# Transposing attention probabilities with VectorE blocks and DMAs instead of TensorE in a two-layer hybrid decoder kernel

## Chip, cores and metric

One core of a Trainium2 chip runs the whole program. The time is that of one execution on the device, in microseconds (us); lower is better. Engines are named as the profile names them: PE is TensorE (PEld its weight loads), DVE is VectorE, ACT is ScalarE, POOL is GpSimd, SP is SyncE, which issues the loads of weights.

## What is computed

Two layers over 256 tokens of width 1024, in float32. Each layer is a half-step feed-forward block, a mixer of three gated branches, and a second half-step feed-forward block, each between RMS norms. The attention of the mixer, cut to what matters:

```
p_s = masked_softmax(q_rot @ k_slc * scale, m_s);  o_s = p_s @ v_slc     # 8 heads of 64, causal
p_w = masked_softmax(q_rot @ k_win * scale, m_w);  o_w = p_w @ v_win
y_nsa = g0 * o_c + g1 * o_s + g2 * o_w             # o_c: over 15 compressed blocks
p_m = softmax(q_m @ k_mem * scale);  y_mem = p_m @ v_mem                 # 4 heads of 128, 256 tokens
merged = g_conv*(y_conv @ w_conv) + g_nsa*(y_nsa @ w_nsa) + g_mem*(y_mem @ w_mem)
```

With 256 tokens and 64-token blocks, the 16 selected blocks are all blocks and the window covers all tokens, so `o_s` and `o_w` are both plain causal attention.

## The kernel before

Tokens are two tiles of 128 (t = 0, 1), each a `stream` that walks feed-forward, mixer, feed-forward for both layers. A product of float32 accuracy is three matmuls of "float32r" parts (`mm3`, L335): high by high, low by high, high by low. So every weight tile (128x1024, 512 KB, loaded by SP into `raw`) is split by ACT into `whi` and by DVE into `wlo` (`split_unit`, L266), and every moving or stationary activation is split too (`evac_split`, L368).

The order is a program of steps. A step is one piece of weight product of one stream, six matmuls in most cases; streams take turns, with t = 0 at most LEAD = 3 steps ahead. `advance` (L318) counts steps, runs what `later` deferred, and splits weights whose use is up to AHEAD = 4 steps off. Beside the streams, up to LANES = 4 chains (`background`, L1132) each advance one piece per step at most: compression, memory, and attention. A chain's `yield n` means: go on n steps later. The scheduler of the tile framework then places instructions within each engine by their readiness; SP's order is as written. Buffers come from rotating pools, `gtile` (19 of 128x1024) and `ttile` (8 of 128x520).

An attention chain has 512 score columns per PSUM bank and two banks. Per layer there are two `nsa_first` (t = 0; 128 keys, both variants of four heads), four `nsa_second` (t = 1; 256 keys, one variant of four heads) and two `mem_attention` (two heads, both t). Each puts its scores on PE, takes the maximum on DVE and the exponent on ACT, multiplies by the reciprocal sum and gate on DVE (L811, L840, L1044), and then needs the probabilities with keys on partitions. For that, PE transposes four 128x128 blocks into a PSUM bank (L779, L1053), ACT and DVE evacuate and split them (`ph`, `pl`), and PE multiplies by the values (L857, L1062). That happens twice in a chain: 32 groups of four transposes in the program. A fifth piece for t = 1 (third for t = 0), `cmp_attention`, adds the compressed branch; the last piece to arrive closes `o`, which ACT and DVE split into `ynsa` (L861). The mixer's branches come in the order convolution, memory, nsa (ORDER), and a stream that needs `ynsa` is held by `("until", ...)` (L1202) until its closing piece has been written into the program.

The feed-forward blocks already transpose without PE, in `turn_beside` (L385): DVE transposes 32x32 blocks, four DMAs issued by POOL write them to DRAM, one DMA brings them back rearranged, ACT and DVE split the result. The steps at which this is written are set by `AWAY, BACK, SPLIT = 1, 3, 8`.

Of the kernel before, what the change touches and what calls it, by code (L numbers as in the profile page):

```python
# [55 lines left out]
DBUFS = 4  # L56
CMP = 4
ATT_A, ATT_B, ATT_C, ATT_D = 1, 3, 2, 3
# [64 lines left out]
def program(nc, pools, a, out, plan):  # L123
# [261 lines left out]
    def turn_beside(src, n, put):  # L385
        c, f = n // P, n // 4
        blocks = gtile("blocks")
# [10 lines left out]
        def back():  # L398
            moved.append(gtile("moved"))
            nc.gpsimd.dma_start(moved[0][:, :n], there[:, :n])  # L400

        def split():
            hi, lo = gtile("turnhi", F32R), gtile("turnlo", F32R)
            dims, r = [[32, c], [f, 4], [1, 32]], "p (c q i) -> p c q i"
            hv, lv = hi[:, :n].rearrange(r, c=c, q=4), lo[:, :n].rearrange(r, c=c, q=4)
            nc.scalar.copy(hv, view(moved[0], 0, dims))  # L406
            nc.vector.tensor_sub(lv, view(moved[0], 0, dims), f32(hv))  # L407
            put(hi, lo)
# [3 lines left out]
        later(SPLIT, split)  # L412
# [234 lines left out]
    def kv_first(t, l, ps, r):  # L647
# [14 lines left out]
        def turn():  # L662
# [54 lines left out]
    def q_part(t, l, ps, r):  # L717
# [18 lines left out]
        def turn(i):  # L736
            def go():
                for half in range(2):
# [29 lines left out]
    def softmax_part(s3, dg, sums, c0, p3):  # L768
# [4 lines left out]
        for i in range(n):  # L773
            nc.scalar.activation(p3[:, i], s3[:, i], AF.Exp, bias=nm[:, i:i + 1], accum_out=sums[:, c0 + i:c0 + i + 1])
# [9 lines left out]
    def weighted_values(t, l, kt, var, g, ph, pl, last):  # L784
        vh, vl = values(kt, var, g)
        accumulate(t, l, 1, [(st, mv[:, :512]) for st, mv in ((vh, ph), (vh, pl), (vl, ph))], last)

    def nsa_first(l, g):
# [3 lines left out]
        pu = []  # L792
        for u in range(2):
# [7 lines left out]
            yield ATT_A  # L801
            s4 = s.rearrange("p (c k) -> p c k", c=4)
            p = ttile("p")
            p4 = p[:, :512].rearrange("p (c k) -> p c k", c=4)
            softmax_part(s4, s4, sums, u * 4, p4)
            pu.append(p4)
        yield ATT_B
        r = recip_gate(sums, 8, view(S["gt"][0], g * 12 + 1, [[3, 4], [1, 2]]))
        for u in range(2):
            for c in range(4):  # L810
                nc.vector.tensor_scalar(pu[u][:, c], pu[u][:, c], r[:, u * 4 + c:u * 4 + c + 1], None, op0=OP.mult)  # L811
        yield ATT_C
        for var in range(2):
            ph, pl = turn_probabilities([pu[h // 2][:, h % 2 * 2 + var] for h in range(4)])
            yield ATT_D
            weighted_values(0, l, 0, var, g, ph, pl, True)

    def nsa_second(l, var, g):
# [4 lines left out]
        pu = []  # L823
        for u in range(2):
# [7 lines left out]
            p = ttile("p")  # L832
            p3 = p[:, :512].rearrange("p (i k) -> p i k", i=2)
            softmax_part(s3, s3[:, :, P:2 * P], sums, u * 2, p3)
            pu.append(p3)
# [452 lines left out]
```

## Time and profile before

| | |
|---|---|
| time, median of 3 runs | 1289.2 us (1287.98 to 1293.4) |
| the profiled execution: time, span | 1287.19 us, 1285.4 us |
| PE busy, matmuls | 1273.1 us (99%), 6026 |
| DVE, ACT, POOL busy | 912.2 (71%), 738.6 (57%), 140.5 us (11%) |
| granted TensorE clock | 0.999 |
| moved by DMA | 263.81 MB, 205 GB/s |

The span is from the first to the last instruction; the execution's own time is 1.8 us longer. Busy shares of PE are modelled (matmuls overlap), so starts of matmuls tell more than busy time. The two layers lie one after the other: the attention chains stand at about 275 to 400 us and 910 to 1035 us.

### The profile page before, as it was taken

The numbers are of one execution on the slowest core, as the hardware profiler recorded it, in microseconds if no ns is written. First come the engines' busy times: TensorE is split into PE (matmuls) and PEld (weight loads), VectorE is DVE, ScalarE is ACT, GpSimd is POOL, SyncE is SP. The second block draws the span as 40 slices with busy tenths as digits, with TensorE's granted clock in tenths as the row PEclk, the third lists the DMA queues.
The fourth block names the chain that finished last, engine by engine and source line by source line (L and its number), as shares of the span: only waits on it lengthen the run. The fifth ranks groups of instructions, "written<-read, shape, count | busy, mean of one in ns | idle before, by whom it ended". The sixth has DMA issues, their size and how long they took to land.

```text
span 1285.4 us, 17101 instructions
## 1 busy us (share of the span) xinstructions
PE 1273.1 (99%) x6026; PEld 1055.2 (82%) x6026; DVE 912.2 (71%) x1352; ACT 738.6 (57%) x1175; POOL 140.5 (11%) x304
## 2 busy tenths in 40 slices
PE   9999999999999999999999999999999999999998
PEld 7888888888888888888888888888888888888886
DVE  6767467889877666676565765579997866766753
ACT  6655466886655464554464555568866555645541
POOL 3101401200000010111011011013000000110110
PEclk9999999999999999999999999999999999999999
DMA  8777585764555657787757776757654456577772
GB/s 265 245 248 252 188 271 172 220 213 131 151 155 161 206 180 199 254 257 244 231 175 240 220 248 229 240 167 233 184 151 144 132 180 211 179 216 236 254 247 81
DMA packets 126502, 263.81 MB, mean 205 GB/s; under 512 B 10097, under 2 KB 29201, under 8 KB 126417
## 3 DMA queue, kind: packets, MB, share of 16 engines
q1 hardware_dynamic: 118256, 239.30, 60.0%
q0 software_dynamic: 8128, 23.41, 5.4%
q8 instruction: 47, 0.77, 0.2%
q14 instruction: 39, 0.31, 0.1%
q10 hardware_dynamic: 32, 0.01, 0.0%
HBM read 250.10 MB, written 12.58 MB: 204 GB/s over the span
## 4 chain that ended last, share of the span: by engine, by line
PE 89%; DVE 4%; DMA 3%; ACT 2%; issue 1%; POOL 1%; DVEq 0%; POOLq 0%; ACTq 0%
PE acc L336 19%; PE acc L337 19%; PE acc L338 19%; PE y L338 6%; PE y L337 6%; PE y L336 6%; PE pt L379 2%; PE br L336 2%; PE br L337 2%; PE br L338 2%; PE o L857 1%; DMA there<-blocks 1%; DVE wlo L275 1%; PE pt L779 1%; DMA raw<-in_w_mix_in_dram 1%
## 5 line engine op out<-in xcount | busy, mean ns | idle before, releaser
L278 ACT ACTIVATE whi<-raw,gT 128x512 fp32r<-128x512 f32 (+2 forms) x432 | 364.5, 873 | 248.4 <-PE acc L338 167.1
L279 DVE SCALAR_TENSOR_TENSOR wlo<-raw,gT,whi 128x512 fp32r<-128x512 f32 (+2 forms) x432 | 396.4, 937 | 155.8 <-ACT whi L278 154.6
L336 PE MATMUL acc<-whi,hThi 128*128 128x512 f32 (+1 forms) x1184 | 464.1, 393 | 0.8 <-ACT hThi L370 0.8
L337 PE MATMUL acc<-wlo,hThi 128*128 128x512 f32 (+1 forms) x1184 | 458.5, 388 | 0.1
L338 PE MATMUL acc<-whi,hTlo 128*128 128x512 f32 (+1 forms) x1184 | 457.8, 388 | 0.0
L338 PEld LDWEIGHTS acc<-whi,hTlo 128*128 128x128 f32 x1184 | 222.2, 188 | 45.7 <-DVE hTlo L371 0.3
L336 PEld LDWEIGHTS acc<-whi,hThi 128*128 128x128 f32 x1184 | 222.4, 188 | 43.9 <-ACT hThi L370 1.6
L337 PEld LDWEIGHTS acc<-wlo,hThi 128*128 128x128 f32 x1184 | 222.6, 188 | 42.1 <-DVE wlo L279 0.6
L275 DVE TENSOR_TENSOR wlo<-raw,whi 128x1024 fp32r<-128x1024 f32 x144 | 175.2, 1222 | 79.3 <-ACT whi L274 78.0
L274 ACT CAST whi<-raw 128x1024 fp32r<-128x1024 f32 x144 | 150.3, 1051 | 104.9 <-PE acc L338 57.3
L337 PE MATMUL y<-wlo,turnhi 128*128 128x512 f32 x352 | 137.6, 391 | 0.1
L338 PE MATMUL y<-whi,turnlo 128*128 128x512 f32 x352 | 137.5, 391 | 0.0
L336 PE MATMUL y<-whi,turnhi 128*128 128x512 f32 x352 | 136.3, 390 | 0.0
L393 POOL DMA_DIRECT2D there<-blocks x96 | 53.0, 558 | 314.8 <-DVE blocks L388 312.0
L423 POOL TENSOR_TENSOR nr<-nv,mhalf 128x1 f32<-128x1 f32 x28 | 19.1, 682 | 545.4 <-DVE nv L421 541.4
L337 PEld LDWEIGHTS y<-wlo,turnhi 128*128 128x128 f32 x352 | 66.1, 188 | 14.4 <-DVE wlo L275 1.0
L338 PEld LDWEIGHTS y<-whi,turnlo 128*128 128x128 f32 x352 | 66.1, 188 | 13.5
L336 PEld LDWEIGHTS y<-whi,turnhi 128*128 128x128 f32 x352 | 66.0, 188 | 13.6
L407 DVE TENSOR_TENSOR turnlo<-moved,turnhi 128x1024 fp32r<-128x1024 f32 (+1 forms) x24 | 27.2, 1135 | 58.2 <-ACT turnhi L406 50.9
L406 ACT CAST turnhi<-moved 128x1024 fp32r<-128x1024 f32 (+1 forms) x24 | 23.4, 977 | 67.2 <-DMA moved<-there 44.6
L488 ACT ACTIVATE th<-acc,rs 128x512 f32<-128x512 f32 (+1 forms) x48 | 31.0, 645 | 17.5 <-PE acc L338 17.5
L493 DVE SCALAR_TENSOR_TENSOR wide<-th,rs,acc 128x512 f32<-128x512 f32 (+1 forms) x48 | 33.6, 701 | 2.9 <-DVE th L489 0.2
(292 smaller groups left out, 1232.6 us busy)
## 6 DMA issues: line engine op xcount, KB each, us to landing
raw<-in_ffn_w_in_dram SPq DMA_DIRECT2D x160, 512.0 KB, 4.8
raw<-in_w_mix_in_dram SPq DMA_DIRECT2D x96, 512.0 KB, 3.7
raw<-in_ffn_w_out_dram SPq DMA_DIRECT2D x88, 512.0 KB, 4.7
there<-blocks POOLq DMA_DIRECT2D x64, 128.0 KB, 5.2
moved<-there POOLq DMA_DIRECT2D x16, 512.0 KB, 5.8
raw<-in_ffn_w_in_dram SPq DMA_DIRECT2D x32, 256.0 KB, 4.0
raw<-in_w_mem_kv_dram SPq DMA_DIRECT2D x16, 512.0 KB, 4.9
raw<-in_w_mix_out_dram SPq DMA_DIRECT2D x16, 512.0 KB, 4.3
```

What stands on the lines that cost most here:

```text
L274: nc.scalar.copy(h, v)
L275: nc.vector.tensor_sub(w, v, f32(h))
L278: nc.scalar.activation(h, v, AF.Copy, scale=g)
L279: nc.vector.scalar_tensor_tensor(w, v, g, f32(h), op0=OP.mult, op1=OP.subtract)
L336: nc.tensor.matmul(ps, lhsT=xh, rhs=wh, start=start, stop=False, skip_group_check=skip)
L337: nc.tensor.matmul(ps, lhsT=xh, rhs=wl, start=False, stop=False, skip_group_check=skip)
L338: nc.tensor.matmul(ps, lhsT=xl, rhs=wh, start=False, stop=stop, skip_group_check=skip)
L379: nc.tensor.transpose(pt[:, j * P:(j + 1) * P], src[:, c0 + j * P:c0 + (j + 1) * P], ident)
L393: nc.gpsimd.dma_start(there[:, q * f:(q + 1) * f].rearrange("(p j) f -> j p f", j=32), blocks[q * 32:(q + 1) * 32, :n].rearrange("j (p f) ...
L407: nc.vector.tensor_sub(lv, view(moved[0], 0, dims), f32(hv))
L488: nc.scalar.activation(th[:, :n], pa[:, :n], AF.Tanh, scale=r_half)
L493: nc.vector.scalar_tensor_tensor(both[:, c0:c0 + n], th[:, :n], r2_half, pb[:, :n], op0=OP.mult, op1=OP.mult)
```

## The change

The probabilities of all three kinds of chain go through `turn_beside` in one 128x1024 tile per chain, and TensorE's 128 transposes for them are gone: 6026 matmuls become 5898. The scale by reciprocal sum and gate moves from DVE to ACT, as do the copies of `G` (`kv_first`) and `QT` (`q_part`) that DVE made. The split of the turned tile is written 10 steps after the block transpose (`ATT_T`), the products with the values 5 steps later (`ATT_D`). Chains of "nsa" and "memory" start at least 9 steps apart (`PACE`). The pool of DRAM buffers has 8 instead of 4.

```diff
-DBUFS = 4
+DBUFS = 8
-ATT_A, ATT_B, ATT_C, ATT_D = 1, 3, 2, 3
+ATT_A, ATT_B, ATT_C, ATT_D, ATT_T = 1, 3, 2, 5, 10
+CHAINS = 3, 5
+PACE, PACED = 9, ("nsa", "memory")
...
-                        eng = nc.scalar.copy if g == 0 else nc.vector.tensor_copy
+                        eng = nc.scalar.copy
...
-                    if half == 0:
-                        nc.scalar.copy(dst, pt)
-                    else:
-                        nc.vector.tensor_copy(dst, pt)
+                    nc.scalar.copy(dst, pt)
...
-    def turn_probabilities(parts):
-        pt = tbank()
-        for c, part in enumerate(parts):
-            nc.tensor.transpose(pt[:, c * P:(c + 1) * P], part, ident)
-        ph, pl = ttile("ph", F32R), ttile("pl", F32R)
-        evac_split(ph[:, :512], pl[:, :512], pt)
-        return ph, pl
...
+    def attend_values(t, l, parts):
+
+        def put(hi, lo):
+            def go():
+                for n, (half, kt, var, g) in enumerate(parts):
+                    ph, pl = [v[:, half * 512:(half + 1) * 512] for v in (hi, lo)]
+                    c = var * 512 + g * 128
+                    vh, vl = vz[kt][:, c:c + 128], vz[kt][:, c + 256:c + 384]
+                    accumulate(t, l, 1 / len(parts), [(vh, ph), (vh, pl), (vl, ph)])
+            later(ATT_D, go)
+        return put
...
     def nsa_second(l, var, g):
...
-        pu = []
+        p = gtile("p")
...
-        for h in range(4):
-            part = pu[h // 2][:, h % 2]
-            nc.vector.tensor_scalar(part, part, r[:, h:h + 1], None, op0=OP.mult)
+        for k in range(4):
+            part = view(p, k * P, [[512, 2], [1, P]])
+            nc.scalar.activation(part, part, AF.Copy, scale=r[:, k:k + 1])
         yield ATT_C
-        for kt in range(2):
-            ph, pl = turn_probabilities([pu[h // 2][:, h % 2, kt * P:(kt + 1) * P] for h in range(4)])
-            yield ATT_D
-            weighted_values(1, l, kt, var, g, ph, pl, kt == 1)
...
+        turn_beside(p, 1024, attend_values(1, l, [(kt, kt, var, g) for kt in range(2)]), ATT_T)
...
     def background():
-        while pending and len(lanes) < LANES:
+        while pending and len(lanes) < LANES and (pending[0][0][0] not in PACED or now[0] >= paced[0]):
             key, task = pending.pop(0)
+            if key[0] in PACED:
+                paced[0] = now[0] + PACE
             lanes.append([now[0], key, task])
```

`nsa_first` and `mem_attention` are changed in the same way (eight 128x128 scalings in the former). `turn_beside` itself keeps its work and gets a `wait` argument.

In the built program, **PE's queue** at the first chain of layer 0 before: the products of one half with the values (`o<-ph`), then the four transposes (`pt<-ident,p`) of the other half, between weight products.

```order
L338 MATMUL acc<-whi,hTlo 128x512
L857 MATMUL o<-ph,vz_123 128x512
L857 MATMUL o<-pl,vz_123 128x512
L857 MATMUL o<-ph,vz_123 128x512
L779 MATMUL pt<-ident,p 128x128 x4
L336 MATMUL acc<-whi,hThi 128x512
L337 MATMUL acc<-wlo,hThi 128x512
L338 MATMUL acc<-whi,hTlo 128x512
```

And with the change, at the products of the first chain:

```order
L804 MATMUL s<-KTh,QT_2375 128x256
L804 MATMUL s<-KTl,QT_2375 128x256
L856 MATMUL o<-turnhi,vz_123 128x512
L856 MATMUL o<-turnlo,vz_123 128x512
L856 MATMUL o<-turnhi,vz_123 128x512 x2
L856 MATMUL o<-turnlo,vz_123 128x512
L856 MATMUL o<-turnhi,vz_123 128x512
L338 MATMUL acc<-whi,hThi 128x512
L339 MATMUL acc<-wlo,hThi 128x512
L340 MATMUL acc<-whi,hTlo 128x512
```

The transposes are gone, and both halves' products stand together, right behind the scores (`s`) of the second chain.

**POOL's queue** before, at the end of the rotary embedding of t = 1 and at the convolution's small copies (`vT`, `carry`) up to the mixer's post-norm (`nr`):

```order
L725 TENSOR_TENSOR qr<-ra_2513,rb_2514 128x8x8
L726 TENSOR_TENSOR qr<-ra_2513,rb_2514 128x8x8
L1081 MEMSET vT 128x4x2
L1087 COPY carry<-vT 128x8
L1084 COPY vT<-carry 128x4x2
L423 TENSOR_TENSOR nr<-nv,mhalf 128x1 x2
```

With the change:

```order
L733 TENSOR_TENSOR qr<-ra_2513,rb_2514 128x8x8
L734 TENSOR_TENSOR qr<-ra_2513,rb_2514 128x8x8
L396 DMA there<-blocks 32x4x256 x4
L1077 MEMSET vT 128x4x2
L403 DMA moved<-there 128x1024
L396 DMA there<-blocks 32x4x256
L1083 COPY carry<-vT 128x8
L396 DMA there<-blocks 32x4x256 x3
L1080 COPY vT<-carry 128x4x2
L403 DMA moved<-there 128x1024
L396 DMA there<-blocks 32x4x256 x4
L403 DMA moved<-there 128x1024
```

Eight round trips of four DMAs out (`there`) and one back (`moved`) now stand in a queue that had nothing there but three small operations; the last of these three stands behind the first chain's way back, which waits for its way out.

**PE's queue** at the end of layer 0's attention before, where the nsa branch of t = 1 (`br<-whi,ynsa`) first meets its input; the closing product of that input stands 72 matmuls ahead of it:

```order
L338 MATMUL acc<-whi,hTlo 128x512
L336 MATMUL acc<-whi,hThi 128x512
L337 MATMUL acc<-wlo,hThi 128x512
L338 MATMUL acc<-whi,hTlo 128x512
L336 MATMUL br<-whi,ynsa 128x512
L337 MATMUL br<-wlo,ynsa 128x512
L338 MATMUL br<-whi,ynsa 128x512
L336 MATMUL br<-whi,ynsa 128x512
L337 MATMUL br<-wlo,ynsa 128x512
L338 MATMUL br<-whi,ynsa 128x512
```

With the change (`o<-phc` is that closing product, of the compressed branch; its four transposes `pt<-ident,pc` stand seven matmuls ahead of it, and 26 matmuls ahead of those the last of its scores):

```order
L340 MATMUL acc<-whi,hTlo 128x512
L338 MATMUL acc<-whi,hThi 128x512
L339 MATMUL acc<-wlo,hThi 128x512
L856 MATMUL o<-phc,vst 128x512
L340 MATMUL acc<-whi,hTlo 128x512
L338 MATMUL acc<-whi,hThi 128x512
L339 MATMUL acc<-wlo,hThi 128x512
L340 MATMUL acc<-whi,hTlo 128x512
L338 MATMUL br<-whi,ynsa 128x512
L339 MATMUL br<-wlo,ynsa 128x512
L338 MATMUL acc<-whi,hThi 128x512
L340 MATMUL br<-whi,ynsa 128x512
```

Four matmuls are left between the closing product and the first that needs its result.

## Rows read from the trace of the kernel before

**Rows 1.** The page: span, and each engine's busy time.
```profile
span 1285.4 us, 17101 instructions
...
PE 1273.1 (99%) x6026; PEld 1055.2 (82%) x6026; DVE 912.2 (71%) x1352; ACT 738.6 (57%) x1175; POOL 140.5 (11%) x304
```

**Rows 2.** Stretches: PE, PEld, DVE, ACT, POOL busy, clock, DMA share, GB/s.
```profile
225.00:275.00 50.00, 49.01 (x299) 42.08 (x298) 44.72 (x79) 41.41 (x82) 11.75 (x18) 1.00 0.78 238
...
275.00:345.00 70.00, 70.00 (x368) 58.48 (x367) 61.73 (x151) 48.32 (x123) 0.76 (x3) 1.00 0.48 142
345.00:430.00 85.00, 85.00 (x415) 70.81 (x414) 65.02 (x119) 48.64 (x87) 0.00 (x0) 1.00 0.56 161
...
465.00:640.00 175.00, 175.00 (x778) 145.00 (x777) 114.14 (x114) 88.44 (x97) 19.52 (x36) 1.00 0.74 232
```

**Rows 3.** Timeline of PE (start, us): first and last group of transposes.
```profile
290.61 0.39 PE L338 MATMUL acc<-whi,hTlo 128*128 128x512 f32 x1
290.84 0.60 PE L779 MATMUL pt<-ident,p 128*128 128x128 f32 x4
291.20 0.48 PE L336 MATMUL acc<-whi,hThi 128*128 128x512 f32 x1
291.51 0.40 PE L337 MATMUL acc<-wlo,hThi 128*128 128x512 f32 x1
...
1026.10 0.60 PE L779 MATMUL pt<-ident,p 128*128 128x128 f32 x4
```

**Rows 4.** Chain of waits, 275 to 430 us: shares, one group of transposes.
```profile
by line: PE acc L336 20.6%; PE acc L338 20.3%; PE acc L337 20.1%; PE br L336 6.2%; PE br L337 5.9%; PE br L338 5.9%; PE o L857 5.7%; PE pt L779 3.4%; PE s L829 2.4%; PE om L1062 1.8%; PE pt L379 1.5%; PE s L798 1.2%; PE pt L1053 1.1%; PE sc
...
291.00 0.44 PE pt L779 x4
```

**Rows 5.** Groups of PE by line: the removed transposes.
```profile
L779 PE MATMUL pt<-ident,p 128*128 128x128 f32 x96 | 14.4, 272 | 0.0
...
L1053 PE MATMUL pt<-ident,pm 128*128 128x128 f32 x32 | 4.8, 272 | 0.0
```

**Rows 6.** Groups of DVE by form: count, busy us, mean ns.
```profile
L388 DVE STREAM_TRANSPOSE blocks<-wide 128x1024 f32<-128x1024 f32 x16 | 19.8, 1237 | 0.0
L407 DVE TENSOR_TENSOR turnlo<-moved,turnhi 128x1024 fp32r<-128x1024 f32 x16 | 19.6, 1223 | 33.3 <-ACT turnhi L406 26.0 <-DMA there<-blocks 7.3
L371 DVE TENSOR_TENSOR pl<-pt,ph 128x512 fp32r<-128x512 f32 x24 | 16.4, 685 | 3.3 <-ACT ph L370 3.1
...
L840 DVE TENSOR_SCALAR p<-p,rg 128x256 f32<-128x256 f32 x32 | 9.3, 348 | 0.2
...
L811 DVE TENSOR_SCALAR p<-p,rg 128x128 f32<-128x128 f32 x32 | 6.9, 279 | 0.1
...
L974 DVE TENSOR_TENSOR sc<-sc,cmadd 128x128 f32<-128x128 f32 x4 | 1.1, 287 | 0.2
```

**Rows 7.** Groups of ACT by form, idle before each behind the bar.
```profile
L406 ACT CAST turnhi<-moved 128x1024 fp32r<-128x1024 f32 x16 | 16.8, 1048 | 33.8 <-DMA moved<-there 33.8
...
L774 ACT ACTIVATE p<-s,nm 128x256 f32<-128x256 f32 x32 | 14.9, 476 | 0.0
L370 ACT CAST ph<-pt 128x512 fp32r<-128x512 f32 x24 | 13.9, 580 | 14.4 <-PE pt L779 14.4
L774 ACT ACTIVATE p<-s,nm 128x128 f32<-128x128 f32 x32 | 11.4, 381 | 1.2 <-DVE nm L772 1.2
...
L406 ACT CAST turnhi<-moved 128x768 fp32r<-128x768 f32 x8 | 6.7, 836 | 33.3 <-issue 12.5 <-DMA moved<-there 10.8 <-DMA there<-blocks 10.0
```

**Rows 8.** Tile blocks: the DMA out, issue ns (min/median/max) and landing.
```profile
L393 POOL DMA_DIRECT2D there<-blocks x96: 552/552/641, 55.3 to 1229.2; - x96
...
DMA to landing us min/median/max: 2.8/5.0/7.4
```

**Rows 9.** Tile moved: the DMA back, likewise.
```profile
L400 POOL DMA_DIRECT2D moved<-there x24: 555/567/577, 62.6 to 1236.7; - x24
...
DMA to landing us min/median/max: 3.3/5.1/8.4
```

More of the change, by code (lines that the diff above doesn't have):

```diff
@@ L398, in back, with quarters, turn_beside, split @@
         def back():
-            moved.append(gtile("moved"))
+            moved.append(make("moved"))
             nc.gpsimd.dma_start(moved[0][:, :n], there[:, :n])
[L402 to L408, printed above, removed]
         later(AWAY, away)
         later(BACK, back)
-        later(SPLIT, split)
+        later(wait, lambda: finish(view(moved[0], 0, [[32, c], [f, 4], [1, 32]])))
+    def quarters(ap, c):
+        return ap if dry else ap.rearrange("p (c q i) -> p c q i", c=c, q=4)
+    def turn_beside(src, n, put, wait=SPLIT):
+        def split(mv):
+            hi, lo = gtile("turnhi", F32R), gtile("turnlo", F32R)
+            hv, lv = quarters(hi[:, :n], n // P), quarters(lo[:, :n], n // P)
+            nc.scalar.copy(hv, mv)
+            nc.vector.tensor_sub(lv, mv, f32(hv))
+            put(hi, lo)
+        turn(src, n, split, wait)
     def rstd(halves):
@@ L766, in values, with softmax_part @@
         return vz[t][:, c:c + 128], vz[t][:, c + 256:c + 384]
-    def softmax_part(s3, dg, sums, c0, p3):
+    def softmax_part(s3, dg, sums, place):
         n = s3.shape[1] if not dry else 1
@@ L852, in accumulate @@
         o = S["o"][t]
-        if last:
-            S["parts"][t] += 1
-        closing = last and S["parts"][t] == 5
+        S["parts"][t] += share
+        closing = S["parts"][t] == CHAINS[t]
         for n, (st, mv) in enumerate(products):
@@ L1018, in mem_attention @@
         scale = 128.0 ** -0.5
-        pm = []
+        p = gtile("pm")
+        sums = sp.tile([P, 4], F32, name="sumsm")
         for t in range(2):
@@ L1039, in mem_attention @@
         yield ATT_B
-        for p3, sums in pm:
-            r = sp.tile([P, 2], F32, name="rm")
-            nc.vector.reciprocal(r, sums)
-            for i in range(2):
-                nc.vector.tensor_scalar(p3[:, i], p3[:, i], r[:, i:i + 1], None, op0=OP.mult)
-        yield ATT_C
-        o = bank("om")
-        o3 = o.rearrange("p (i q) -> p i q", i=2)
-        for kt in range(2):
-            pt = tbank()
-            for i in range(2):
-                for t in range(2):
-                    c = i * 2 + t
-                    nc.tensor.transpose(pt[:, c * P:(c + 1) * P], pm[t][0][:, i, kt * P:(kt + 1) * P], ident)
-            ph, pl = ttile("phm", F32R), ttile("plm", F32R)
-            evac_split(ph[:, :512], pl[:, :512], pt)
-            yield ATT_D
-            vm = S["vm"][kt]
-            for i in range(2):
-                h = 2 * u + i
-                vh, vl = vm[:, h * P:(h + 1) * P], vm[:, 512 + h * P:512 + (h + 1) * P]
-                for n, (st, mv) in enumerate(((vh, ph), (vh, pl), (vl, ph))):
-                    nc.tensor.matmul(o3[:, i], lhsT=st, rhs=mv[:, i * 256:(i + 1) * 256],
-                                     start=(kt == 0 and i == 0 and n == 0), stop=(kt == 1 and i == 1 and n == 2),
-                                     skip_group_check=True)
@@ L1065, in mem_attention, with put, go @@
-        y = [t[:, u * 512:(u + 1) * 512] for t in S["ymT"]]
-        evac_split(y[0], y[1], o)
-        S["mparts"] += 1
-        if S["mparts"] == 2:
-            S["ymem"] = True
+        r = sp.tile([P, 4], F32, name="rm")
+        nc.vector.reciprocal(r, sums)
+        for k in range(4):
+            part = view(p, k * P, [[512, 2], [1, P]])
+            nc.scalar.activation(part, part, AF.Copy, scale=r[:, k:k + 1])
+        def put(hi, lo):
+            def go():
+                o = bank("om")
+                o3 = o.rearrange("p (i q) -> p i q", i=2)
+                for kt in range(2):
+                    ph, pl = [v[:, kt * 512:(kt + 1) * 512] for v in (hi, lo)]
+                    vm = S["vm"][kt]
+                    for i in range(2):
+                        h = 2 * u + i
+                        vh, vl = vm[:, h * P:(h + 1) * P], vm[:, 512 + h * P:512 + (h + 1) * P]
+                        for n, (st, mv) in enumerate(((vh, ph), (vh, pl), (vl, ph))):
+                            nc.tensor.matmul(o3[:, i], lhsT=st, rhs=mv[:, i * 256:(i + 1) * 256],
+                                             start=(kt == 0 and i == 0 and n == 0),
+                                             stop=(kt == 1 and i == 1 and n == 2), skip_group_check=True)
+                y = [t[:, u * 512:(u + 1) * 512] for t in S["ymT"]]
+                evac_split(y[0], y[1], o)
+                S["mparts"] += 1
+                if S["mparts"] == 2:
+                    S["ymem"] = True
+            later(ATT_D, go)
@@ L1071, in conv_part @@
+        yield ATT_C
+        turn_beside(p, 1024, put, ATT_T)
     def conv_part(t, l, u_s, c_ps, r):
```

55 lines of the change are left out of this document (23 added, 32 removed).

## The prediction

> **What bounds the kernel now.** Read the page's busy times first [rows 1]: PE is busy 1273.1 of 1285.4 us, DVE 71%, ACT 57%. As busy time of PE is modelled, check it where the change acts: in the table of stretches [rows 2] PE has no idle time from 275 to 430 us (70.00 of 70.00, 85.00 of 85.00), with DVE at 88% and 76% and the DMAs at about half, against 0.74 in a feed-forward stretch. Then look at starts [rows 3]: matmuls of 512 columns start 0.23 us apart (290.61, 290.84). This is the pitch of PE, and nothing but PE sets it. The chain of waits agrees [rows 4]: over these 155 us its shares all stand at PE lines. So in this stretch a microsecond of PE work removed is one gained, as long as what replaces it arrives in time.
>
> **What is removed from PE.** A group of four transposes starts at 290.84 us, the next matmul at 291.20, and the one after that at 291.51 instead of 0.23 us later [rows 3]: 0.36 + 0.08 = 0.44 us, which is also what the chain of waits gives such a group [rows 4]. The program loses 96 + 32 = 128 transposes [rows 5], in 32 groups from 290.84 to 1026.10 us [rows 3]: 32 x 0.44 = **14.1 us**. A second way to it: L779 and L1053 hold 3.4% + 1.1% of the 155 us [rows 4], 7.0 us a layer, 14.0 for two. No other matmul goes or comes.
>
> **What is moved between DVE and ACT, per layer.** DVE loses 16 scalings of 0.279 us, 16 of 0.348 and the memory chains' 8 (taken at 0.348 too), and 16 splits of 0.685; it gains 8 block transposes of 1.237 and 8 splits of 1.223 [rows 6]. 23.8 go, 19.7 come: -4 us, of some 127 busy in 275 to 430 us [rows 2]. ACT loses 16 evacuations of 0.580 and gains 8 of 1.048, 16 scalings of 128x128 (nearest row: the exponent of that size, 0.381) and 24 of 256 columns (0.476) [rows 7]: +17 us, on some 97 busy [rows 2]. 114 of the 148 us that would then be left is 77%: no new bound. The copies of `G` and `QT` that ACT takes over, 8 of at most 0.381 and 4 of about 0.58 [rows 7], add 5 us in 225 to 275 us, where ACT is busy 41.4 of 50 us [rows 2]. I cost this at nothing, since 8.6 us are idle there; if ACT's queue then holds up weight splits, PE's idle time there, now 1.0 us, may double, +1 us a layer.
>
> **What the new way costs, and what covers it.** One chain's round trip, by rows: block transpose 1.24 [rows 6], four issues of 0.55 on POOL = 2.2, landing 5.0 [rows 8], one issue 0.57, landing 5.1 [rows 9]: 14.1 us. Then 1.05 on ACT and 1.22 on DVE [rows 7, 6]: 16.4 us until PE may multiply. Against that stand ATT_T + ATT_D = 15 steps of six matmuls of 0.23 us, 20.7 us, and more where other chains' matmuls lie between. The cover leaves 4.3 us. With each landing the longest on record (7.4 and 8.4 us [rows 8, 9]) the way takes 22.1 us, 1.4 too many.
>
> What queues behind the new wait is the weight splits on ACT: the split of the turned tile is written 10 steps = 13.8 us after the block transpose, against 14.1 us, so ACT would stand 0.3 us at its head. The feed-forward blocks show that such a stand is free: their split comes after 8 steps = 11.0 us, so that by the same sum ACT should stand 3.1 us; its idle time there is (33.8 + 33.3) / 24 = 2.8 us [rows 7], and PE loses nothing by it (175.00 of 175.00 busy [rows 2]). On POOL a chain takes 2.2 + 5.0 + 0.57 = 7.8 us, and chains start 9 steps = 12.4 us apart, so round trips don't pile up. The convolution's copies (`vT`, `carry`) stand behind one such trip, at most 7.8 us later; between the transposes that feed them and the branch that needs them lie some 70 matmuls (16 us), so I cost this at nothing. DMA bytes rise by 16 x 1 MB where the DMAs are half idle [rows 2].
>
> The DMA issues themselves: 96 on POOL took 0.552 us in the median and 0.641 at most [rows 8], though DVE was busy most of the time beside them; by these rows five issues are 2.8 us a chain. [...]
>
> **The end of each layer's attention** is the tight place. Chains now start later and last longer, and the piece that closes `ynsa` for t = 1 comes right before its user: 26 matmuls (6.0 us) from the last compressed scores to their transposes, 7 (1.6 us) on to the product, 4 (0.9 us) on to the first use; before, 72 lay in the last gap. The first gap holds some 12 small dependent operations on DVE and ACT, at 0.287 each [rows 6] 3.4 us, plus 0.4 for the last matmul to end; but each can queue behind a weight split of 1.2 us, and two of these fill the gap. The second and third hold 0.58 on ACT and 0.685 on DVE each [rows 7, 6], with nothing to spare. So PE stands between 0 and 3 us a layer; I take 1.0, nearer to the lower end because the sums fit without queueing. **+2.0 us.**
>
> **The sum.** -14.1 + 2.0 = -12.1 us. The profiled execution took 1287.2 us, so 1275.1 against its own; the median of the runs shown is 2.0 us higher, so **1277 us** against that.
>
> **The rivals.**
> 1. *The ends of attention cost more*, 2 to 4 us a layer, because small operations queue behind two or three splits each: -14.1 + 6 = -8, 1281 us. For it: gaps of 4 and 7 matmuls. Against: DVE and ACT have idle time there.
> 2. *Nothing comes of it*, because DVE paces this stretch and not PE: 1289 us. For it: DVE at 88% in 275 to 345 us. Against: PE without idle time in the same stretch [rows 2], starts at pitch right behind a group [rows 3], and DVE loses work too.
> 3. *Slower: the products wait for the round trip.* Place: the first `o<-turnhi` of each of 16 chains. It decides from landings of 14.4 us together on (20.7 - 6.3 of fixed work); to eat the whole gain takes 12.1 / 16 = 0.76 us a chain, landings of 15.2 together against medians of 10.1. With all at their longest, 15.8, it is 16 x 1.4 = 22 us: 1277 + 22 = 1299. Against: the DMAs have less to do here than in the feed-forward stretches from which these landings come [rows 2].
> [...]
> That the change doesn't do what it says is excluded on PE by the order: 5898 matmuls, no transposes of `p` or `pm`.
>
> **How the numbers follow.** About 0.5% (6.4 us) can be told from no change. Forecast 0.70, its own range 1273 to 1280 (0 to 3 us a layer at the ends, and 1 us for what the medians of runs scatter); rival 1 0.14, of which 0.04 ends within 0.5%; rival 2 0.08; rival 3 0.06; rival 4 0.02. Faster by over 0.5%: 0.70 + 0.10, and 0.02 of rival 2 where it holds for one stretch only: 0.82. Within: 0.04 + 0.06 = 0.10. Slower: 0.08. The range reaches to 1284, which takes in rival 1, and down to 1272: the full 14.1 us and 3 more if PE's idle microseconds around DVE's removed work go too.
>
> **What would show it right or wrong.** Right: PE still without idle time in the attention stretch, no `pt<-ident,p`, ACT's idle before `turnhi` of attention under 2 us a chain, landings of `there` and `moved` near 5 us, and idle time of PE before `pt<-ident,pc`, `o<-phc` and `br<-whi,ynsa` of 0 to 3 us a layer. Wrong: PE waiting for `turnhi` or `turnlo` at `o` or `om`, POOL issues of over 1 us, ACT over 90% from 275 on, or weight matmuls that wait for `whi` behind an ACT that stands.

## The result, and the profile after

The changed kernel takes 1282.1 us (median of 14 runs, 1278.6 to 1286.3), the kernel before, run beside it, 1288.6 (14 runs, 1286.5 to 1293.4): a ratio of 0.994, 95% interval 0.9924 to 0.9957. It is faster, by about half of what was forecast: 6.5 us instead of 12.1. The time lies in the range of 1272 to 1284. The profiled execution took 1282.4 us, its span 1280.5.

Where the change acts, the forecast held. Three answers of the trace of after: the busy times of the page, the table of stretches (columns as in [rows 2]; the last is 5 us earlier than there), and the landing of the DMA out of `blocks` from 275 to 430 us.

```profile
PE 1259.4 (98%) x5898; PEld 1043.1 (81%) x5898; DVE 900.4 (70%) x1244; ACT 770.7 (60%) x1263; POOL 182.1 (14%) x384
```

```profile
225.00:275.00 50.00, 49.21 (x301) 42.43 (x300) 40.69 (x67) 44.50 (x92) 11.84 (x21) 1.00 0.78 241
275.00:345.00 70.00, 70.00 (x358) 58.93 (x357) 63.23 (x125) 60.29 (x150) 13.24 (x26) 1.00 0.71 221
345.00:430.00 85.00, 85.00 (x394) 69.78 (x393) 66.04 (x108) 54.08 (x97) 9.37 (x18) 1.00 0.71 213
460.00:635.00 175.00, 175.00 (x778) 145.04 (x777) 113.00 (x114) 86.94 (x96) 19.58 (x37) 1.00 0.74 234
```

```profile
DMA to landing us min/median/max: 2.3/3.3/5.4
```

PE is again without idle time from 275 to 430 us, with 128 matmuls fewer in the whole program; the DMAs have gone from half busy to 0.71, and their transfers land early all the same. ACT waits only 1.0 us in that stretch for its eight turned tiles, in all (groups by line, 275 to 430 us, of after):

```profile
L417 DVE TENSOR_TENSOR turnlo<-moved,turnhi 128x1024 fp32r<-128x1024 f32 x8 | 9.7, 1216 | 0.1
...
L416 ACT CAST turnhi<-moved 128x1024 fp32r<-128x1024 f32 x8 | 8.4, 1052 | 1.0 <-DMA moved<-there 1.0
```

To see where the rest went, the program is cut at five places that both kernels have: the last matmul ahead of the transposes of `x` with which a norm opens, where PE always waits 0.2 to 0.3 us. Between these starts of PE lie the stages; the first stage begins with PE's first transpose (`pt<-ident,first`), and the end is what comes after the start of the last matmul. In us, from the profiled executions (the runs below this line in the table are those of the experiments; "drain" is explained under the table):

| kernel | setup and ffn1, layer 0 | mixer 0 | ffn1, layer 1 | mixer 1 | end | GpSimd transfers | drain | median, runs |
|---|---|---|---|---|---|---|---|---|
| before | 206.9 | 246.8 | 207.0 | 246.5 | 6.3 | 138 | 2.80 | 1288.6, 14 |
| after | 208.1 | 239.0 | 211.3 | 238.9 | 11.3 | 218 | 9.17 | 1282.1, 14 |
| after, second trace | 213.8 | 238.9 | 212.1 | 239.1 | 11.3 | 218 | 9.17 | 1289.1, 1 |
| after, third trace | 208.7 | 238.9 | 210.1 | 240.1 | 11.3 | 218 | 9.17 | 1282.8, 6 |
| before, no transposes | 206.9 | 239.3 | 206.2 | 239.4 | 6.4 | 138 | 2.80 | 1272.3, 4 |
| before, 80 large transfers | 207.1 | 251.7 | 207.0 | 251.6 | 11.3 | 218 | 9.17 | 1303.9, 4 |
| before, 80 small transfers | 207.1 | 248.6 | 206.3 | 248.9 | 10.7 | 218 | 8.60 | 1295.5, 1 |
| after, writes by ScalarE | 207.7 | 247.8 | 206.3 | 246.7 | 6.8 | 154 | 4.11 | 1291.9, 10 |
| after, writes by SyncE | 210.8 | 244.2 | 206.3 | 247.8 | 6.7 | 154 | 4.11 | 1286.1, 10 |
| after, SPLIT 11 | 214.2 | 240.4 | 208.2 | 238.9 | 11.3 | 218 | 9.17 | 1287.7, 10 |
| after, ATT_T 6 | 209.5 | 259.4 | 214.5 | 259.4 | 11.5 | 218 | 9.17 | 1327.9, 1 |
| after, 30 small transfers | 210.5 | 239.1 | 206.3 | 240.1 | 13.2 | 248 | 11.05 | 1282.4, 12 |
| after, last roots moved | 207.3 | 239.1 | 208.5 | 240.1 | 6.4 | 218 | 9.15 | 1276.6, 6 |
| the same, constants by SyncE | 207.3 | 238.8 | 207.7 | 239.1 | 6.8 | 201 | 8.50 | 1272.5, 4 |

The two second feed-forwards (181.8 and 183.6 us) are the same in nearly all of them and are left out. From before to after: the mixers give 7.8 + 7.6 = 15.4 us, and 1.2 + 4.3 + 5.0 = 10.5 us are lost elsewhere, together 4.9, the difference of the spans.

**The end.** In both traces the queue of each of the five engines ends with DRAIN instructions and semaphore events, here called the closing barrier. The DRAINs on the queues of GpSimd and SyncE (durations in ns, minimum, median, maximum; start of the first and the last), of before and of after:

```profile
L1284 POOLq DRAIN  x3: 46/93/2803, 1280.4 to 1285.2; - x3
L1284 SPq DRAIN  x3: 7/7/7, 1284.6 to 1284.9; - x3
```

```profile
L1282 POOLq DRAIN  x3: 46/93/9170, 1270.6 to 1280.3; - x3
L1282 SPq DRAIN  x3: 7/7/7, 1274.8 to 1280.0; - x3
```

GpSimd's long DRAIN starts in both 1.3 us after the start of the last matmul, together with its last power. Before, it was over at 1283.2, ahead of SyncE, which reached the barrier at 1284.6. After, SyncE is there at 1274.8 and waits 5.0 us, until 1279.8.

**Layer 1's first feed-forward.** GpSimd's timeline of after in that stage (start, us; the idle time ahead and what ended it in brackets), and of before in layer 1's second feed-forward:

```profile
684.66 2.26 POOL L396 DMA_DIRECT2D there<-blocks  x4 [37.13 <-DVE blocks L391]
692.03 0.58 POOL L403 DMA_DIRECT2D moved<-there  x1 [5.11 <-PE acc L340]
695.59 2.20 POOL L396 DMA_DIRECT2D there<-blocks  x4 [2.97 <-issue]
703.29 0.56 POOL L403 DMA_DIRECT2D moved<-there  x1 [5.50 <-DMA there<-blocks]
```

```profile
1188.22 0.56 POOL L393 DMA_DIRECT2D there<-blocks  x1 [26.02 <-DVE blocks L388]
1191.39 1.65 POOL L393 DMA_DIRECT2D there<-blocks  x3 [2.60 <-issue]
```

"Issue" says that GpSimd waited for nothing that the profile shows; its blocks were written. Each kernel makes this pause of 2.4 to 3.0 us once where the trace lets it be told: the kernel before following its 119th transfer, the changed one following its 121st. The 40 additional transfers of layer 0 have moved it ahead by 496 us. What it does in after, from the timelines of PE, ACT and DVE, and the clock in the table of stretches:

```profile
709.55 0.39 PE L340 MATMUL acc<-whi,hTlo 128*128 128x512 f32 x1
710.15 1.04 ACT L416 CAST turnhi<-moved 128x1024 fp32r<-128x1024 f32 x1 [3.78 <-DMA moved<-there]
...
711.23 1.22 DVE L417 TENSOR_TENSOR turnlo<-moved,turnhi 128x1024 fp32r<-128x1024 f32 x1 [3.54 <-ACT turnhi L416]
...
712.37 0.74 DVE L501 SCALAR_TENSOR_TENSOR wide<-th,rs,acc 128x512 f32<-128x512 f32 x1
...
713.16 0.54 PE L338 MATMUL acc<-whi,hThi 128*128 128x512 f32 x1 [3.23 <-DVE wide L501]
```

```profile
705.00:709.50 4.50, 4.50 (x21) 3.74 (x20) 1.28 (x1) 1.15 (x1) 0.00 (x0) 1.00 0.91 320
...
713.20:717.00 3.80, 3.80 (x10) 2.98 (x11) 3.58 (x4) 1.15 (x1) 0.00 (x0) 0.55 0.12 24
```

The round trip that starts with blocks at 691.3 gets to its split 18.9 us later, with 8 steps (11 us) of cover; ACT and DVE stand at their queues' heads, the evacuation behind them doesn't come, and PE stands 3.2 us. Then the granted clock is 0.55: matmuls start 0.43 us apart (713.93, 714.36), and 10 go in 3.8 us where 16 or 17 would at the pitch of 0.23: another 1.5 us.

**The setup.** PE waits there for small constants that GpSimd loads between round trips: 0.4 us in before, 1.4, 5.2 and 1.7 us in the three traces of after. The first 1236 rows of PE's order are the same in both programs, and up to the first landmark the rows of all engines come in the same order in both traces, so no way is seen by which the change would reach this stage. The wait differs from run to run; but the four traces of kernels built from before have 206.9 to 207.1 us here, and the nine of kernels built from after that load these constants on GpSimd have 207.3 to 214.2. So chance alone isn't shown, and the cause stays open (the eight DRAM buffers instead of four were not tried by themselves).

### The profile page after: what moved, and what is told of

It reads as the page before. It is cut to its first block, busy times and chain, and to the rows that moved or that the text cites. A ratio compares the mean times of both kernels' runs of the same rounds, so it can differ in the third digit from the quotient of the medians.

```text
span 1280.5 us, 16988 instructions
## 1 busy us (share of the span) xinstructions
PE 1259.4 (98%) x5898; PEld 1043.1 (81%) x5898; DVE 900.4 (70%) x1244; ACT 770.7 (60%) x1263; POOL 182.1 (14%) x384
## 4 chain that ended last, share of the span: by engine, by line
PE 89%; DMA 3%; ACT 2%; DVE 2%; issue 1%; POOL 1%; DVEq 0%; POOLq 0%; ACTq 0%
PE acc L338 19%; PE acc L340 19%; PE acc L339 19%; PE y L340 7%; PE y L339 6%; PE y L338 6%; PE pt L381 2%; DMA there<-blocks 2%; PE br L338 2%; PE br L340 2%; PE br L339 2%; PE o L856 1%; DMA moved<-there 1%; ACT whi L280 1%; PE s L834 1%
## 5 line engine op out<-in xcount | busy, mean ns | idle before, releaser
L396 POOL DMA_DIRECT2D there<-blocks x160 | 87.9, 556 | 475.3 <-DVE blocks L391 472.0
L417 DVE TENSOR_TENSOR turnlo<-moved,turnhi 128x1024 fp32r<-128x1024 f32 (+1 forms) x40 | 46.8, 1169 | 69.7 <-ACT turnhi L416 69.5
L416 ACT CAST turnhi<-moved 128x1024 fp32r<-128x1024 f32 (+1 forms) x40 | 40.3, 1008 | 79.4 <-DMA moved<-there 62.9
L403 POOL DMA_DIRECT2D moved<-there x40 | 22.4, 561 | 188.4 <-DMA there<-blocks 131.9
```

The lines of the kernel that those rows point to most:

```text
L396: nc.gpsimd.dma_start(there[:, q * f:(q + 1) * f].rearrange("(p j) f -> j p f", j=32), blocks[q * 32:(q + 1) * 32, :n].rearrange("j (p f) ...
L416: nc.scalar.copy(hv, mv)
L417: nc.vector.tensor_sub(lv, mv, f32(hv))
```

## The experiments

All ratios are to the kernel before, run beside each. Twelve experiments were made; the last two give a version faster than both kernels. Three of them (the first repeat, the small transfers of 3, and 6) have a single run, and are used for their traces.

**1. The changed kernel again**, unchanged, twice (one run; six).

> The changed kernel once more, unchanged, for a second trace. If the 9.17 us that GpSimd's DRAIN took at the program's end belongs to the change, it is again 8 to 10 us here. If TensorE's stand of 3.2 us in layer 1's first feed-forward (at 709.55) and the 1.40 us at the transposes of the staged rows (at 149.88) are lateness of a transfer by chance, they are not both here again: the stand is under 1 us or in another place. If they belong to the change, both are within 0.5 us of what they were. Time 1277 to 1286 us either way.

> The changed kernel unchanged once more, timed beside the kernel with the 30 small transfers on the same chip. Theory: the drain is 9.2 us and TensorE's stand after the 121st transfer 2.7 to 3.3 us again; the setup's length (206.9 us in the kernel before, 208.1 and 213.8 us in the two traces of the changed one, with the same order of TensorE's first 1236 rows) differs by chance. Median 1280 to 1286 us, 3 to 9 us below the kernel before.

Drain 9.17 us each time. The stand in layer 1's first feed-forward is there each time, in the same place, with 2.7 and 2.0 us; the setup's waits vary (5.2 and 1.7 us). The six runs have a ratio of 0.9943 (0.992 to 0.9966), as at first. So end and stand belong to the change. The setup's lateness varies from run to run, and 5.2 us of it stand in the one run of 1289.1, above the expected range.

**2. Before without its transposes.**

```diff
-    def turn_probabilities(parts):
-        pt = tbank()
-        for c, part in enumerate(parts):
-            nc.tensor.transpose(pt[:, c * P:(c + 1) * P], part, ident)
+    def turn_probabilities(part):
...
-        evac_split(ph[:, :512], pl[:, :512], pt)
+        evac_split(ph[:, :512].rearrange(r, a=a), pl[:, :512].rearrange(r, a=a), part)
```

> The kernel before without the 128 TensorE transposes of the attention probabilities and nothing in their place: the split into the two halves reads the probabilities as they stand, so they reach the products untransposed. It leaves the transposition out. Theory (a transpose that goes gives back its whole 0.11 us, since TensorE is what bounds a mixer): each layer's mixer is 7.0 us shorter, 239.8 and 239.5 us, and the time is 14 us below the kernel before, 1274 to 1275. Rival (VectorE bounds part of the stretch): under 10 us in all, 1279 or more, with new waits of TensorE in the attention. The end of the program is as before, its drain 2.8 us.

The mixers fall by 7.5 and 7.1 us, layer 1's first feed-forward by 0.8, nothing else moves, the drain is 2.80; ratio 0.9861 (0.9828 to 0.9895). The first term of the sum is right to within 0.5 us, and VectorE doesn't pace the stretch.

**3. Before with 80 more transfers**, large and small. The scheduler put most of them not where the chains stand but at the start of each mixer, as soon as `x` was ready.

```diff
+        def sh_away():
+            for q in range(4):
+                nc.gpsimd.dma_start(sh[:, q * 256:(q + 1) * 256].rearrange("(p j) f -> j p f", j=32),
+                                    x[0][q * 32:(q + 1) * 32, :].rearrange("j (p f) -> j p f", p=4))
+        def sh_back():
+            unread = gtile("unread")
+            nc.gpsimd.dma_start(unread, sh[:, :])
```

> The kernel before with the changed kernel's 80 additional GpSimd transfers and nothing else of it: each of the 16 chains of a layer's attention also writes 512 KB of the resident x to a DRAM scratch tile in four issues and reads it back in one into a tile that nothing reads. Theory: GpSimd's DRAIN at the end grows with the transfers that GpSimd has issued in the whole program, so it takes 9 us here instead of 2.8, the barrier waits for it, and the time is that of the kernel before plus 5 us, 1293 to 1295 us, with layer times of the mixers within 0.5 us of before's 246.8 and 246.5. Rival: the drain is set by something else that the change brought (the buffer count of the DRAM pool, the order at the end, chance); then it stays at 2.8 us and the time at 1288 to 1290 us.

> The kernel before with 80 additional GpSimd transfers at the places where the other kernel of this kind had its 64 of 128 KB and 16 of 512 KB, each of one row of 512 bytes. If the drain and the pause go by the number of transfers, the drain is 9.2 us again and the pause comes after 119 to 121 of them, in layer 1's first feed-forward. If they go by bytes or by rows moved, the drain is 2.8 to 3.5 us and the pause stands in layer 1's second feed-forward as in the kernel before. The mixers, 251.7 and 251.6 us with the large transfers against 246.8 and 246.5 without, tell whether those 5 us a layer were the traffic (then 247 here) or the issues on GpSimd's queue (then 251 to 252 here).

The large ones: drain of 9.17 us, as after's, end 11.3, pause of 2.66 us following the 121st transfer; ratio 1.0104 (1.0071 to 1.0137). The small ones: 8.60 us, pause following the 128th. So both follow the number of transfers and not their bytes in the main; where the rest comes from is told under 7. The kernel with the large ones is slower than the 1293 to 1295 us expected: of its 14 us, 5 are at the end and 4.9 + 5.1 in the mixers, where this experiment's own bunching does harm. PE waits 3.1 us in each for `zc` (6.1, 2 times in the waits of PE, against 1.3 in before); the rest of the mixers' loss is not traced. The changed kernel has no such wait. With small ones, in a single trace, the mixers lose 1.8 and 2.4 us, so over half of that loss goes with the size of the transfers.

```profile
L1302 POOLq DRAIN  x3: 46/98/9173, 1290.0 to 1299.7; - x3
```

**4. The attention's writes issued by another engine.**

```diff
+        far = nc.scalar if wait == ATT_T else nc.gpsimd
...
-                nc.gpsimd.dma_start(there[:, q * f:(q + 1) * f].rearrange("(p j) f -> j p f", j=32),
+                far.dma_start(there[:, q * f:(q + 1) * f].rearrange("(p j) f -> j p f", j=32),
```

> The changed kernel with the 64 DRAM writes of the attention's round trips issued by ScalarE instead of GpSimd, one step later each, as is the read back. Theory (drain grows with GpSimd's own issues, 138 to 218 giving 2.8 to 9.2 us): with 154 of them the drain is 3 to 5 us and hidden behind SyncE's last waits, and the time falls by 4 to 5 us to 1277 to 1278. Rival (the drain depends on the bytes or the descriptors moved, whoever issues them, or on something else): 9 us again and 1282. If ScalarE's issues cost it 0.4 us each in its stream, that is 1.6 us a chain on an engine with 30 to 40 percent of idle time, and TensorE's mixers stay within 1 us of 239.0 and 238.9 us.

> The changed kernel with the 64 DRAM writes of the attention's round trips issued by SyncE, in the place where GpSimd issued them. GpSimd has 154 transfers in all, as in the kernel with ScalarE's issues, so the drain is 4.1 us and hidden, and the pause after 119 to 121 transfers falls into layer 1's attention or later, where a round trip has 15 steps of cover. Theory: the 5.0 us at the end and the 3 to 4 us in layer 1's first feed-forward are both given back, with nothing taken from ScalarE: 1273 to 1275 us. Rival: a write that waits for its blocks holds the weight loads behind it on SyncE's queue, TensorE waits for a weight in the mixers, and they become 1 to 4 us a layer longer: 1276 to 1282.

With 154 transfers on GpSimd the drain is 4.11 us and hidden, the end 6.8 and 6.7, and layer 1's first feed-forward 206.3 us without a stand, as expected. But the mixers lose all of it: ratios 1.0016 (0.9998 to 1.0034) by ScalarE, 0.9973 (0.9954 to 0.9992) by SyncE, and neither time is the one expected. That an issue costs ScalarE 0.4 us was the author's assumption; what these issues took of its queue is in no view shown here. PE waits for what comes late from ScalarE and VectorE (waits of PE, writes by ScalarE):

```profile
PE s L835 <- ACT gth L1195: 3.7, 2, 1.9
PE o L857 <- DVE phc L994: 3.3, 2, 1.6
```

On SyncE an issue took 434 ns in the median (327 to 602), and the writes stand for their blocks ahead of the weight loads (waits of SP, 275 to 430 us):

```profile
SPq L397 <- DVE blocks L392: 68.9, 8, 16.3
```

The rival of SyncE's run was right, and worse than it said: +5 and +9 us of mixer, with PE waiting for `whi` and `wlo` up to 1.0 us at a time.

**5. Three more steps for the feed-forward's round trips**, `SPLIT = 11` instead of 8.

> The changed kernel with 11 steps instead of 8 between the DVE blocks of a feed-forward's round trip and its split (the attention's chains keep their 10). In all six traces so far GpSimd makes one pause of 2.6 to 3.0 us, for which no wait is shown, after its 119th to 121st transfer, whatever the kernel; the 80 more transfers have moved it from layer 1's second feed-forward (1188.8 us in the kernel before) into a round trip of layer 1's first feed-forward (692.6 us). Theory: TensorE's stand of 3.2 and 2.7 us in that feed-forward is this pause, seen because the round trip had no steps to spare; with three more (4 us) the pause is still there at 119 to 121 transfers and the stand is gone, the stretch between the ends of feed-forwards 207.0 to 207.5 us as in the kernel before instead of 211.3 and 212.1, and the time 3 to 4 us below the changed kernel, 1278 to 1279. Rival: the stand comes from the weights' transfers or from VectorE, and it stays within 1 us of 3. The drain stays 9.2 us.

The pause is there (2.89 us), the stand 1.7 us instead of 2.0 to 3.2, smaller but not gone: a trip of 18.9 us wants 14 steps of 1.38 us and not 11 (an estimate from the trace of after). New waits came with the later splits (1.0 us in layer 0's first feed-forward, 1.4 us in mixer 0), and the ratio is 0.9983 (0.9963 to 1.0004), so nothing is won. Why its median is 5.6 us above the changed kernel's, where 3 to 4 us below it were expected, isn't settled; 2.9 us in its trace are a late constant.

**6. Four steps less for the attention's round trips**, `ATT_T = 6` instead of 10.

> The changed kernel with 6 steps instead of 10 between an attention chain's DVE blocks and the split: 11 steps to the products instead of 15, 15.2 us by the prediction's 1.38 us a step against a round trip of 16.4 us there. If the prediction's cover is right and near its edge, the split now waits for its read back on ScalarE in most chains and TensorE stands 1 to 3 us in a few of the 16, so that each mixer is 1 to 6 us above 239. If the round trip is shorter than was reckoned, the mixers stay within 0.5 us of 239.0 and 238.9.

Both mixers are 20.4 us longer, far beyond the 1 to 6 us expected. Waits of PE from 275 to 430 us:

```profile
PE o L856 <- ACT turnhi L416: 7.8, 3, 3.7
PE om L1054 <- ACT turnhi L416: 4.8, 1, 4.8
```

PE stands 12.6 us in layer 0, and the granted clock is down there: 0.89 in the mean from 330 to 345 us and from 365 to 380. By that some 3 of the other 7.8 us are the clock's (an estimate: 0.11 of these 30 us); the rest is not traced. So 11 steps are too few; 12 to 14 were not tried.

**7. Thirty small transfers where GpSimd is idle**, 10 ahead of layer 1's first round trip, 20 after the last.

```diff
+            if (l, t, which, j) == (1, 0, 1, 0):
+                pads(10, th)
...
+                    if (l, t, which, j) == (DEPTH - 1, 1, 2, 5):
+                        pads(20, f32(lo))
```

> The changed kernel with 30 more GpSimd transfers of 512 bytes, put where GpSimd is idle and nobody waits for it: 10 ahead of layer 1's first round trip (the 117th to 126th transfer) and 20 after the last round trip, 248 in all. Theory: GpSimd settles its transfers in a pause that comes by their count, first after 119 to 128, then about 103 later, and the drain at the end settles those since the last pause at 0.08 us each. Then the first pause falls among the first 10, TensorE's stand of 2.7 to 3.3 us in layer 1's first feed-forward is gone (206.2 to 207.1 us between the landmarks instead of 211.3 to 212.1), a second pause falls at or after the 222nd transfer, at the end of the last round trip or among the last 20, and the drain is 1 to 4.2 us and hidden instead of 9.2 us: 7 to 9 us below the changed kernel, 1272 to 1278. Rivals: with no second pause the drain is 0.08 us x (248 - 103) = 11.6 us and only the stand's 3 us are won, less 2.4 us at the end; if the stand has another cause, it stays and the time rises by 2.4 us.

GpSimd's timeline:

```profile
687.16 1.14 POOL L401 DMA_DIRECT2D there<-blocks  x2 [19.70 <-DVE blocks L396]
691.00 1.09 POOL L401 DMA_DIRECT2D there<-blocks  x2 [2.71 <-issue]
695.15 0.57 POOL L408 DMA_DIRECT2D moved<-there  x1 [3.05 <-DMA raw<-in_ffn_w_in_dram]
```

The pause moved ahead by only one round trip, to the first of two, and that is enough: no stand, 206.3 us. So the stand is the pause's. A second pause did not come, and the drain grew to 11.05 us: that a second pause follows some 103 transfers after the first is wrong. Ratio 0.9949 (0.9928 to 0.9969): about 4 us are won in this stage, 1.9 given back at the end, and the median of 1282.4 is that of the changed kernel beside it (1282.8), not the 1272 to 1278 expected.

The theory's other half holds: the drain goes by the transfers issued after the pause, not by all in the program. Put side by side from the table and the timelines of GpSimd:

| kernels | transfers | pause following | transfers after the pause | drain, us | 1.25 + 0.0817 for each after the pause |
|---|---|---|---|---|---|
| before; before without transposes | 138 | 119th | 19 | 2.80 | 2.80 |
| before, 80 small transfers | 218 | 128th | 90 | 8.60 | 8.60 |
| after (three traces), and four others built from either kernel | 218 | 121st | 97 | 9.15 to 9.17 | 9.17 |
| after, 30 small transfers | 248 | 128th | 120 | 11.05 | 11.05 |
| constants by SyncE (8 below) | 201 | 112th | 89 | 8.50 | 8.52 |

```profile
L1301 POOLq DRAIN  x3: 46/93/8602, 1284.1 to 1293.2; - x3
L1293 POOLq DRAIN  x3: 46/98/11050, 1269.2 to 1280.8; - x3
L1286 POOLq DRAIN  x3: 46/98/8498, 1223.7 to 1271.2; - x3
```

The line is an estimate, laid through the first and the third row; the other three were not used for it. By the number in the whole program the last row would be 7.8 us, the second 9.2 and the fourth 11.6. With 154 transfers the pause can't be told from a longer idle time at the 119th; 35 after it would give 4.11, as measured.

**8. The last two roots away from GpSimd**, and then also the 17 small constant loads.

```diff
-        nc.gpsimd.tensor_tensor(r, v, mhalf, op=OP.pow)
+        if last:
+            nc.scalar.activation(v, v, AF.Sqrt)
+            nc.vector.reciprocal(r, v)
+        else:
+            nc.gpsimd.tensor_tensor(r, v, mhalf, op=OP.pow)
```

> The changed kernel with the root of the last two norms (one of each row half) on ScalarE and VectorE (Sqrt, reciprocal) instead of GpSimd's power. GpSimd's last work is then the last round trip at about 1227 us. Theory: the drain of 9.2 us is the settlement of GpSimd's own transfers and needs nothing else, so it starts as soon as GpSimd has no more work, still takes 9.2 us, and is over long before the last matmul; the 5.0 us by which SyncE waited for it at the end are won, less up to 0.5 us for the longer root: 1277 to 1279 us, 4.5 to 5 us below the changed kernel. TensorE's stand of 2 to 3.3 us in layer 1's first feed-forward stays. Rival: the drain waits for the end of the other engines or of the last transfers, and the end stays 11 us long after the last matmul: 1282.

The drain still takes 9.15 us, but from 1222.4 us on, beside the last matmuls; the end is 6.4 us as in before. Ratio 0.991 (0.9882 to 0.9937), 1276.6 us: 5.5 below the changed kernel's median (3.9 by the two ratios). So the 5.0 us at the end were this drain and nothing else.

```profile
L1286 POOLq DRAIN  x3: 46/93/9152, 1222.4 to 1273.0; - x3
```

```diff
-            nc.gpsimd.dma_start(rest[i * 16:(i + 1) * 16, 0:P], a[PRE[i + 1]].rearrange("l (k p) -> (l k) p", p=P))
+            nc.sync.dma_start(rest[i * 16:(i + 1) * 16, 0:P], a[PRE[i + 1]].rearrange("l (k p) -> (l k) p", p=P))
```

(and the same for `stage` and `w2s`)

> The same with the 17 small constant loads of GpSimd's queue (3 of norm gains, 10 of staged rows, 4 of compression weights) issued by SyncE. GpSimd has 201 transfers. Theory: the pause comes after its 119th to 121st, now four round trips later than in the changed kernel, between 743 and 775 us; where it falls on the first of two close round trips, as in the kernel with the small transfers, TensorE does not stand, and layer 1's first feed-forward is 206.2 to 207.1 us instead of 210.1 to 212.1. The constant loads no longer stand behind round trips, so TensorE's waits of 1.4 to 5.2 us for them in the setup become under 0.5 us and the setup 206.9 to 207.5 us instead of 208.1 to 213.8. Together 1271 to 1275 us. Rivals: the pause falls on the second of two close round trips and the stand is there in another place (1275 to 1278); the loads delay the weights on SyncE's queue (a wait of TensorE for a weight in the setup).

GpSimd's timeline, the pause now following the 112th transfer, in a round trip that has room:

```profile
727.03 0.56 POOL L396 DMA_DIRECT2D there<-blocks  x1 [25.70 <-DVE blocks L391]
730.03 1.65 POOL L396 DMA_DIRECT2D there<-blocks  x3 [2.44 <-issue]
```

No wait for a constant in the setup, no stand over 0.5 us in layer 1's first feed-forward, the end 6.8 us. **1272.5 us** (1271.2 to 1274.9), ratio **0.9865** (0.9845 to 0.9885): 9.5 us below the changed kernel, near the 10.5 us that were lost outside the mixers. The trace of the version before it, with the roots alone moved, had no wait for a constant either (setup 207.3 us in both), so what moving the constants is worth in the setup these traces don't show.

## Why the prediction was half right

- *PE bounds the attention stretch, and a transpose that goes gives its whole time back* (-14.1 us). Right. Without transposes and without anything in their place the mixers gave 14.6 us, with the whole change 15.4, 14.3 in the third trace. PE still has no idle time there, as in [rows 2].
- *ACT +17 us, DVE -4 us a layer at no cost.* From 275 to 430 us ACT rose by 114.4 - 97.0 = 17.4 us and DVE by 2.5, but that stretch now holds some 3% more of the mixer. Between the landmarks of mixer 0, before and after (columns as in [rows 2]):

```profile
213.39:460.18 246.79, 245.35 (x1272) 204.81 (x1270) 199.66 (x388) 162.08 (x330) 18.12 (x35) 1.00 0.58 174
214.63:453.63 239.00, 237.71 (x1207) 198.21 (x1206) 194.29 (x334) 178.79 (x374) 38.96 (x75) 1.00 0.70 215
```

  DVE falls by 5.4 us, and ACT rises by 16.7, copies of `G` and `QT` included, for which 17 + 5 had been reckoned. Neither became the bound.
- *The copies of `G` and `QT`, nothing or up to 1 us a layer.* The upper end came: eight copies stand in one row on ACT for 1.7 us, `kd` comes late to GpSimd, and PE waits 0.7 us in each layer for it (1.4, 2 times in the waits of PE). The waits for `zc` and `FHL` that before had there, 1.3 + 0.5 us in both layers, went, so it comes out even.
- *A round trip of 16.4 us under 20.7 us of cover.* Right: 3.3 us for the landing of the write in layer 0 instead of 5.0, no wait of PE for `turnhi`, and ACT's stand over eight chains 1.0 to 4.2 us a layer in the three traces, where 0.3 each had been reckoned. With four steps less, 15.2 us, PE did wait, so the way is longer than that in some chains; the price of 41 us in all is many times what the shortfall of 1.2 us would suggest. Rivals 2 and 3 did not happen.
- *GpSimd's issues stay short while DVE works.* Right: 160 issues of `there` with 642 ns at most, 551 in the median, in an execution with DVE busy for 70%; before, 96 with 641 at most and 552. No run shows an issue lengthened by VectorE's work, the term on which rival 4, with its chance of 0.02, rested.
- *+2.0 us at the end of each layer's attention.* Mis-sized. No such wait in two traces of after; in the third, 0.5 us at `br<-whi,ynsa` in layer 1 alone, and 0.7 and 0.8 us in the traces with the small transfers and the moved roots. In most the small operations fit into their gaps.
- **The step that failed** is the cost of the transfers themselves: "five issues are 2.8 us a chain", hidden on an idle queue. 80 more of them cost GpSimd that, and two things besides, both far from the attention: a drain that grew from 2.80 to 9.17 us, of which 5.0 us were in nobody's shadow, and the pause that their count brought into a round trip with no steps to spare, 3 to 5 us with the clock behind it. The sum had no term for any stage outside the mixers. Both stood in the trace of before, though not that they go by the number of transfers: a DRAIN of 2.8 us that ended 1.4 us ahead of SyncE, and 2.8 us of GpSimd's idle time ahead of `there` that no wait explains (groups by form, before):

```profile
L393 POOL DMA_DIRECT2D there<-blocks x96 | 53.0, 558 | 314.8 <-DVE blocks L388 312.0 <-issue 2.8
```

The two errors have opposite signs: by the traces the mixers gave 15.4 us instead of 12.1, and 10.5 were lost outside (1.2 of them in the setup, cause open). That the time still fell into the range is luck: its upper end had been drawn for rival 1, which did not happen.

## What to carry to other kernels

A transfer that is hidden where it is issued can still be paid for elsewhere, as here 80 of them with 5.0 us at the end and 3 to 5 us in a feed-forward: look at what its queue does at the program's end and whether a pause moves with its count (here the drain took 0.08 us for each transfer after the pause), and cost the stages that the change doesn't touch by comparing landmarks, not only the stage it aims at. GpSimd's last piece of work came late here and carried its drain of 9.17 us past the end; with that piece on other engines a drain of 9.15 us ran beside the matmuls, and the end took 6.4 us instead of 11.3. Look for the round trip with the shortest cover, also where nothing was changed: 15 steps held in the attention, while 8 steps in an untouched feed-forward became one of the places where the change lost (a stand of 2.0 to 3.2 us), and three more there were not enough (1.7 us).

## What the runs showed of the hardware

All of this is measured in the profiles of the kernels above.

- GpSimd's DRAIN took 2.80, 8.50, 8.60, 9.17 and 11.05 us with 19, 89, 90, 97 and 120 transfers issued after the pause: 0.08 us for each one more, to within 0.02 us in twelve traces, whether they were of 128 KB or of 512 bytes. In the two versions that gave GpSimd no later work it ran beside the matmuls.
- One pause of 2.4 to 3.0 us on GpSimd's queue, following the 112th to 128th transfer, later where more of them are small; it stands at an issue that by the profile waits for nothing. A second was not seen in 248. What GpSimd does in it, and why the drain counts from there, no view shows.
- With 64 of the writes issued by SyncE, an issue took 434 ns in the median (327 to 602), and a write waited for its blocks, ahead of the loads behind it, for up to 16.3 us.
- At stands of PE the granted clock was down: 0.55 in the 3.8 us behind the one of 3.2 us, and 0.89 in two stretches of 15 us in the kernel with `ATT_T = 6`, in which PE was busy for 10.2 and 11.3 us.
